# An S5 table builder with later stores, and with its TensorE part kept out of the output sums

## The chip, the cores and the metric

The kernel runs on one core of a Trainium2 chip. The metric is the device time of one execution in microseconds (us). Engines are named as the profile names them: PE is TensorE's matmul side, PEld its weight load, DVE is VectorE, ACT is ScalarE, POOL is GpSimd, and SP is the engine whose queue (SPq) issues almost all DMAs.

## The reference

Two layers work on x of 512 tokens by 1024 channels. Each layer is a SwiGLU feed-forward (FF1), a token mixer, and a second feed-forward (FF2); each has an RMS norm before and after and a shift, scale and gate from a conditioning vector:

```
c_act = silu(c)
for l in range(2):
    mod = c_act @ w_mod[l] + b_mod[l]      # nine vectors of 1024
    x = x + 0.5 * gt1 * rms_norm(swiglu(modulate(rms_norm(x), sh1, sc1)))     # FF1
    x = x + gt2 * rms_norm(mixer(modulate(rms_norm(x), sh2, sc2)))
    x = x + 0.5 * gt3 * rms_norm(swiglu(modulate(rms_norm(x), sh3, sc3)))     # FF2
swiglu(h) = (silu(h @ w_gate) * (h @ w_up)) @ w_out                            # inner width 2816
```

Half of the mixer is an S5 layer: 32 groups of 16 channels, each with a 64-dimensional complex diagonal state. Its constants (powers of the discretised A, products of these with B and C, and short-time kernels) do not depend on x. They are what the S5 table builder makes ahead of each mixer.

## The kernel before

**Products.** Every 128x128x512 product is done as three matmuls on a high and a low part of both operands (`mm3`, L266 to L268, for input products; `mmo`, L273 to L275, for output sums). A weight unit is a 128x1024 tile. Weights are streamed: `Weights.load` (L216) issues the DMA on SP's queue, ACT makes the high part (`wh`, L223, two casts), DVE the low part (`wl`, L231, two subtractions). The raw tiles have four buffers (pool `raw_p`), and the same four serve the conditioning matrix's tiles (`wm`, L141), each of which DVE multiplies by silu(c) and sums (L143).

**Feed-forward.** `ff` runs three passes over the inner width: 7, 7 and 8 blocks of 128. In a pass it makes the blocks' input products (two weight units and 48 matmuls a block, named `f00i` for FF1 of layer 0, `f02i` for FF2 of layer 0) and then the pass's output sums (`f00o`, `f02o`), 84 matmuls for each half dh of the output channels, over seven weight units in all. The four banks of half 0 come from the pool `psbg`, those of half 1 from `psmm`, which the input products also use. After the sums of pass 1, DVE adds the banks to partial sums in SBUF (`f00pt`, L567); that frees the banks. The first input product of pass 2 (block 14) takes a bank that one of these additions of half 1 frees.

**Side work.** Two generators run beside FF1 of layer 0 (tables of layer 0) and FF2 of layer 0 (tables of layer 1): `gen_mod`, the conditioning tiles, and `gen_prep`, the table builder. `tick`, which is called when an input unit or a unit of output half 1 is fetched, advances the builder by NPREP/40 steps. NPREP is 95 before. So NPREP sets how early in the program each of the builder's steps is written.

**Table builder.** It first makes small powers on DVE, then works through four chunks, `pr00` to `pr03` for layer 0 and `pr10` to `pr13` for layer 1. A chunk loads its parameters (`bc`, L689), makes `w` (L758, L761), `c0r` and `c0n`, `c`, and then `er` and `ei` (L797 to L811) on POOL. `close` of a chunk is run inside the next chunk's steps: it stores `c` (through `diag`, L749), `er` (L696) and `ei` (L697) into a DRAM table, turns w on PE into `mb` banks (L703) which ACT copies to `m` (L704), makes `g` on PE (L708, L709), whose copy `gs` ACT and DVE write (L712, L713), and stores `m` (four DMAs, L749) and `gs` (eight DMAs, L720). The parameter tile, `c0r`, `c0n` and `gs` have one buffer each. At the start of layer 0's tables, four zero stores (L682) clear the table.

**Order.** A scheduler that has its own estimate of durations decides from program order and dependencies the order in which each engine gets its instructions. Each engine, SP among them, then executes that order strictly, and waits at an instruction whose inputs are not there.

Of the kernel before, what the change touches and what calls it, by code (L numbers as in the profile page):

```python
# [16 lines left out]
T = 512  # L17
# [37 lines left out]
def trunk(ctx: ExitStack, tc: tile.TileContext, x_d, c, wmod, wun, vecs, wab, s5p, cst_d, out, depth=2):  # L55
    nc = tc.nc
# [135 lines left out]
    def tick():  # L192
        for e in list(bg):
            e[2] += e[1]
            while e[2] >= 1:
                e[2] -= 1
                if next(e[0], bg) is bg:
                    bg.remove(e)
                    break
# [205 lines left out]

    side = []
    mark = {"n": 0}

    def step():
        mark["n"] += 1  # L410
        while side:
            try:
                next(side[0])
                break
            except StopIteration:
                side.pop(0)
# [67 lines left out]
    def ff(l, s, h):  # L484
        name = f"f{l}{s}"
        part = {}

        def getw(look=LOOK, ticks=True):
            w = W.get(look)
            if ticks:  # L490
                tick()
            return w

        def evac(j, sl, pg, pu, g):
            n = sl.stop - sl.start
            sg = (half if n == HT else slot)(f"{name}sg{j}")
            ACT.activation(sg, pg[:, :n], AF.Silu)  # L497
            DVE.tensor_tensor(sg, sg, pu[:, :n], op=ALU.mult)  # L498
            after["act"] = ACT.copy(g[0][:, sl], sg)
            DVE.tensor_tensor(g[1][:, sl], sg, g[0].bitcast(F32)[:, sl], op=ALU.subtract)  # L500

        g = {}

        def newg(j):
            g[j] = (slot(f"{name}gh{j}", F32R), slot(f"{name}gl{j}", F32R))

        for p, (j0, j1) in enumerate(PASSES):
            nk = j1 - j0
            js = list(range(j0, j1))
            if p == 0 and l == 0 and s == 0:  # L510
                pp = startup(h)
                for j in range(4):
                    newg(j)
                    evac(j, FULL, pp[2 * j], pp[2 * j + 1], g[j])
                js = js[4:]
                rest()
                spread(40, mod=(gen_mod(0, range(16, 72)), 56), prep=(gen_prep(0), NPREP))
            elif p == 0:
                ws = [getw(8 - i, False) for i in range(8)]
                for j in range(4):  # L520
                    newg(j)
                for sl in HALF:
                    for grp in ((0, 1), (2, 3)):
                        pp = [mmps(f"{name}i{i}") for i in range(4)]
                        for k in range(KD):
                            for i, ps in enumerate(pp):
                                mm3(ps[:, :HT], ws[2 * grp[0] + i], k, h[k], sl, k == 0, k == KD - 1)
                                step()
                        with prio(300 if sl.start == 0 else 0):
                            for i, j in enumerate(grp):  # L530
                                evac(j, sl, pp[2 * i], pp[2 * i + 1], g[j])
                    flush()
                js = js[4:]
            if p == 2:
                o = Out(l, s, name + "o", part)
            for j in js:
                newg(j)
                pp = []
                for i in range(2):
                    w = getw()  # L540
                    ps = mmps(f"{name}i{j}")
                    for k in range(KD):
                        mm3(ps, w, k, h[k], FULL, k == 0, k == KD - 1)
                    pp.append(ps)
                evac(j, FULL, pp[0], pp[1], g[j])
            gl = [g.pop(j) for j in range(j0, j1)]
            if p < 2:
                hold = {}
                for dh in range(2):
                    acc = [(mmps if dh else bgps)(f"{name}o{dh}{tg}") for tg in range(4)]  # L550

                    def unit(kk):
                        u, j = divmod(dh * nk + kk, 2)
                        if u not in hold:
                            hold[u] = getw(ticks=dh == 1)
                        return [t[j] for t in hold[u]]

                    seq = [(kk, tg) for kk in range(nk - 3) for tg in range(4)]
                    seq += [(kk, tg) for tg in range(4) for kk in range(nk - 3, nk)]
                    for kk, tg in seq:  # L560
                        mmo(acc[tg], unit(kk), gl[kk], tg, kk == 0, kk == nk - 1)
                        if kk == nk - 1:
                            if p == 0:
                                part[tg, dh] = slot(f"{name}pt{tg}{dh}")
                                ACT.copy(part[tg, dh], acc[tg])
                            else:
                                DVE.tensor_tensor(part[tg, dh], part[tg, dh], acc[tg], op=ALU.add)  # L567
            else:
                tail_ff(o, nk, gl)
        return None if o.last else o.h  # L570

    def gen_prep(l):
# [99 lines left out]
        dram = s5d["t"]  # L672
# [5 lines left out]
        if l == 0:  # L678
            zero = slot("zero")
            POOL.memset(zero, 0.0)  # L680
            for ch in range(4):
                behind(nc.sync.dma_start(out=dram[ch, :, 0:5 * T].rearrange("p (i n) -> p i n", i=5),  # L682
                                         in_=rep(zero, 5)))
# [7 lines left out]

        def close(ch, nm, w, c, er, ei, c0r, c0n, dd, qg, diag):
            wr, wi, cr, cn = w[:, 0:256], w[:, 256:512], c[:, 0:256], c[:, 256:512]
            for i, v in enumerate((cr, cn)):
                diag(2 + i, lambda g: v.rearrange("p (q n) -> p q n", q=4)[64 * g:64 * g + 64])
            nc.sync.dma_start(out=dram[ch, :, 5 * T:6 * T], in_=er)  # L696
            nc.sync.dma_start(out=dram[ch, :, 6 * T:7 * T], in_=ei)  # L697
            yield
            mb = [slot(nm + f"m{i}") for i in range(2)]
            for i, v in enumerate((wr, wi)):  # L700
                ps = bgps(nm + f"mb{i}")
# [15 lines left out]
            for t in range(4):  # L717
                for g in range(2):
                    o = 4 * T + P * t + 64 * g
                    nc.sync.dma_start(out=dram[ch, 64 * g:64 * g + 16 * t + 16, o:o + 64],  # L720
                                               in_=gs[48 - 16 * t:64, 64 * g:64 * g + 64])
            yield

        bc = params(0)
        rest = None
        for ch in range(4):
# [19 lines left out]
            def diag(i, src, ch=ch):  # L746
                for g in range(2):
                    v = dram[ch, 64 * g:64 * g + 64, i * T:i * T + T].rearrange("p (q g n) -> p q g n", q=4, g=2)
                    nc.sync.dma_start(out=v[:, :, g], in_=src(g))  # L749
# [39 lines left out]
            cr, cn = c[:, 0:256], c[:, 256:512]  # L789
# [6 lines left out]
            er, ei = slot(nm + "er"), slot(nm + "ei")  # L796
# [3 lines left out]
            for i in range(7):  # L800
                n = 1 << i
# [18 lines left out]
        yield from rest  # L820

    s5r, s5d, neg = {}, {}, {}
    NPREP = 15 + 4 * 19 + 4

    def gen_s5(l, utc, res, nm0, chunks):
        for ch in chunks:
# [690 lines left out]
    for l in range(depth):  # L1517
# [5 lines left out]
        if l + 1 < depth:  # L1523
            load_vec(l + 1)
            spread(40, mod=(gen_mod(l + 1, range(32)), 32), prep=(gen_prep(l + 1), NPREP))
        h = ff(l, 2, h)
# [106 lines left out]
```

## Time and profile before

| | us |
|---|---|
| median of 3 runs | 2126.64 (2125.35 to 2126.95) |
| profiled execution, its own time | 2125.73 |
| its span in the trace | 2123.7 |
| PE busy | 2048.8 (96% of the span) |
| FF1 of layer 0, output sums of pass 0 / pass 1 | 38.1 / 54.0 |
| idle time of PE in FF1 of layer 0 before `f00o`, `pr01mb`, `pr01g` | 3.6, 2.2, 1.6 |

The profile is of one execution. 2.0 us of that execution's time lie outside of its span. A row of a timeline gives start and duration in us, engine, source line, operation, output and inputs, and in square brackets the idle time of the engine just before it and what ended that idle time. Line numbers are those of the kernel before.

### The profile page before, as it was taken

How to read it: one execution, taken by the hardware profiler on the slowest of the kernel's cores; microseconds unless marked ns; L12 is line 12 of the kernel's file. 1: busy time of each engine (PE TensorE's matmuls, PEld its weight loads, DVE VectorE, ACT ScalarE, POOL GpSimd, SP SyncE). 2: the span in 40 equal slices, each digit the busy share in tenths (PEclk: the TensorE clock that was granted, in tenths of full speed). 3: DMA queues.
4: the chain of work that ended last, by engine and by line, in shares of the span. 5: the costliest groups of instructions: out<-in, count | busy, mean ns of one | idle time of the engine just before them, and what ended most of it. 6: DMA issues, size and time to landing. Idle time of an engine off the chain costs nothing.

```text
span 2123.7 us, 31849 instructions
## 1 busy us (share of the span) xinstructions
PE 2048.8 (96%) x11702; PEld 1742.0 (82%) x11702; DVE 1256.7 (59%) x2936; ACT 888.4 (42%) x1954; POOL 511.4 (24%) x925
## 2 busy tenths in 40 slices
PE   7999899999789999999999999999997999999998
PEld 5888688799678988888888888888986889888886
DVE  8955666863957864555584455568558585324235
ACT  5532323575267732223362222236554674323132
POOL 4067684210421026775010000001123200000001
PEclk9999899999889999999999999999998899999999
DMA  7676667314212335555433455542132122323231
GB/s 291 231 262 194 215 191 234 109 43 147 77 56 70 124 104 179 178 193 172 136 100 129 160 171 183 180 139 80 60 130 85 46 90 90 98 91 129 70 100 50
DMA packets 109697, 286.08 MB, mean 135 GB/s; under 512 B 31154, under 2 KB 32610, under 8 KB 109540
## 3 DMA queue, kind: packets, MB, share of 16 engines
q1 hardware_dynamic: 108388, 282.39, 40.6%
q8 instruction: 92, 1.51, 0.3%
q10 hardware_dynamic: 1152, 1.65, 0.2%
q14 instruction: 65, 0.53, 0.1%
HBM read 267.59 MB, written 16.41 MB: 134 GB/s over the span
## 4 chain that ended last, share of the span: by engine, by line
PE 76%; DVE 14%; DMA 4%; ACT 3%; issue 2%; SPq 0%; POOL 0%; DVEq 0%; ACTq 0%; POOLq 0%
PE f10i L266 4%; PE f10i L267 4%; PE f10i L268 4%; PE f02i L266 4%; PE f02i L268 3%; PE f12i L268 3%; PE f12i L266 3%; PE f12i L267 3%; PE f02i L267 3%; DMA wm<-in_wmod 3%; PE f00i L267 2%; PE f00i L268 2%; PE f00i L266 2%; DVE wl L231 2%; PE f12o L273 1%
## 5 line engine op out<-in xcount | busy, mean ns | idle before, releaser
L231 DVE TENSOR_TENSOR wl<-w,wh 128x512 fp32r<-128x512 f32 x608 | 412.9, 731 | 112.3 <-ACT wh L223 111.0
L223 ACT CAST wh<-w 128x512 fp32r<-128x512 f32 x648 | 357.9, 622 | 80.5 <-DMA w<-in_wun 48.5
L143 DVE SCALAR_TENSOR_TENSOR wm<-wm,cb 128x1024 f32<-128x1024 f32 x128 | 160.7, 1255 | 229.2 <-DMA wm<-in_wmod 228.8
L266 PE MATMUL f10i<-f02ohh,wh 128*128 128x512 f32 (+1 forms) x416 | 150.0, 361 | 2.2 <-DVE f02pt L324 1.6
L267 PE MATMUL f10i<-f02ohl,wh 128*128 128x512 f32 (+1 forms) x416 | 148.9, 358 | 2.1 <-ACT f02ohl L404 2.1
L266 PE MATMUL f02i<-m0ohh,wh 128*128 128x512 f32 (+1 forms) x416 | 148.7, 360 | 0.8 <-ACT f02sg L497 0.8
L266 PE MATMUL f12i<-m1ohh,wh 128*128 128x512 f32 (+1 forms) x416 | 148.0, 358 | 0.8 <-ACT f12sg L497 0.8
L268 PE MATMUL f10i<-f02ohh,wl 128*128 128x512 f32 (+1 forms) x416 | 148.8, 358 | 0.0
L267 PE MATMUL f12i<-m1ohl,wh 128*128 128x512 f32 (+1 forms) x416 | 148.0, 357 | 0.4 <-ACT m1ohl L404 0.4
L267 PE MATMUL f02i<-m0ohl,wh 128*128 128x512 f32 (+1 forms) x416 | 148.1, 357 | 0.4 <-ACT m0ohl L404 0.4
L268 PE MATMUL f02i<-m0ohh,wl 128*128 128x512 f32 (+1 forms) x416 | 147.9, 357 | 0.2 <-DVE wl L231 0.2
L268 PE MATMUL f12i<-m1ohh,wl 128*128 128x512 f32 (+1 forms) x416 | 147.8, 357 | 0.2 <-DVE wl L231 0.2
L267 PE MATMUL f00i<-h0l,wh 128*128 128x512 f32 x344 | 135.1, 393 | 2.0 <-DVE h0l L1488 1.9
L266 PE MATMUL f00i<-h0h,wh 128*128 128x512 f32 x344 | 133.2, 393 | 3.9 <-ACT h0h L1483 3.9
L268 PE MATMUL f00i<-h0h,wl 128*128 128x512 f32 x344 | 134.4, 391 | 0.0
L330 POOL TENSOR_TENSOR f12pt<-f12pt,Gr 128x512 f32<-128x512 f32 x8 | 10.5, 1314 | 402.7 <-ACT scr L329 402.7
L231 POOL TENSOR_TENSOR wl<-w,wh 128x512 fp32r<-128x512 f32 x40 | 53.2, 1349 | 197.2 <-ACT wh L223 157.7
L330 POOL TENSOR_TENSOR f10pt<-f10pt,Gr 128x512 f32<-128x512 f32 x8 | 10.7, 1339 | 361.3 <-ACT scr L329 357.5
L498 DVE TENSOR_TENSOR f12sg<-f12sg,f12i 128x512 f32<-128x512 f32 (+1 forms) x26 | 15.7, 606 | 136.8 <-PE f12i L268 120.8
L266 PEld LDWEIGHTS f10i<-f02ohh,wh 128*128 128x128 f32 x416 | 79.2, 190 | 14.1 <-DVE f02pt L324 1.8
L267 PEld LDWEIGHTS f10i<-f02ohl,wh 128*128 128x128 f32 x416 | 79.3, 191 | 13.5 <-ACT f02ohl L404 2.4
L266 PEld LDWEIGHTS f02i<-m0ohh,wh 128*128 128x128 f32 x416 | 78.2, 189 | 12.8 <-ACT f02sg L497 1.0
(2598 smaller groups left out, 5309.0 us busy)
## 6 DMA issues: line engine op xcount, KB each, us to landing
w<-in_wun SPq DMA_DIRECT2D x324, 512.0 KB, 4.1
wm<-in_wmod SPq DMA_DIRECT2D x128, 512.0 KB, 3.9
wm<-in_wmod SPq DMA_DIRECT2D x32, 256.0 KB, 5.8
s5d<-zero SPq DMA_DIRECT2D x4, 1280.0 KB
Gr<-Gd SPq DMA_DIRECT2D x12, 256.0 KB, 4.1
x<-in_x SPq DMA_DIRECT2D x4, 512.0 KB
m0s0tb<-s5d SPq DMA_DIRECT2D x7, 256.0 KB
m0s1tb<-s5d SPq DMA_DIRECT2D x7, 256.0 KB, 5.5
```

The lines of the kernel that those rows point to most:

```text
L143: DVE.scalar_tensor_tensor(w, w, 1.0, cb, op0=ALU.mult, op1=ALU.mult, accum_out=m)
L223: ACT.copy(hi[j], raw[:, j * T:j * T + T])
L231: e.tensor_tensor(lo[j], raw[:, j * T:j * T + T], hi[j].bitcast(F32), op=ALU.subtract)
L266: PE.matmul(ps, hi, h[0][:, sl], start=start, stop=False)
L267: PE.matmul(ps, hi, h[1][:, sl], start=False, stop=False)
L268: mark["pe"] = PE.matmul(ps, lo, h[0][:, sl], start=False, stop=stop)
L273: PE.matmul(ps, gh, hi, start=start, stop=False)
L330: (POOL if self.part else DVE).tensor_tensor(y, src, self.G[dh], op=ALU.mult)
L498: DVE.tensor_tensor(sg, sg, pu[:, :n], op=ALU.mult)
```

## The change

`close` no longer begins with the stores of `c`, `er` and `ei`; they stand at its end, behind those of `m` and `gs`. Ahead of its PE part it yields as long as a flag says that the output sums of pass 0 or 1 are being written; `ff` sets the flag. NPREP goes from 95 to 109, so that the builder advances 2.725 instead of 2.375 steps a tick. Nothing is added to or taken from the work of any engine.

```
     side = []
     mark = {"n": 0}
+    phase = {"busy": False}
...
             if p < 2:
                 hold = {}
+                phase["busy"] = True
                 for dh in range(2):
...
                                 DVE.tensor_tensor(part[tg, dh], part[tg, dh], acc[tg], op=ALU.add)
+                phase["busy"] = False
             else:
                 tail_ff(o, nk, gl)
...
         def close(ch, nm, w, c, er, ei, c0r, c0n, dd, qg, diag):
             wr, wi, cr, cn = w[:, 0:256], w[:, 256:512], c[:, 0:256], c[:, 256:512]
-            for i, v in enumerate((cr, cn)):
-                diag(2 + i, lambda g: v.rearrange("p (q n) -> p q n", q=4)[64 * g:64 * g + 64])
-            nc.sync.dma_start(out=dram[ch, :, 5 * T:6 * T], in_=er)
-            nc.sync.dma_start(out=dram[ch, :, 6 * T:7 * T], in_=ei)
-            yield
+            while phase["busy"]:
+                yield
             mb = [slot(nm + f"m{i}") for i in range(2)]
...
                                                in_=gs[48 - 16 * t:64, 64 * g:64 * g + 64])
+            yield
+            for i, v in enumerate((cr, cn)):
+                diag(2 + i, lambda g: v.rearrange("p (q n) -> p q n", q=4)[64 * g:64 * g + 64])
+            nc.sync.dma_start(out=dram[ch, :, 5 * T:6 * T], in_=er)
+            nc.sync.dma_start(out=dram[ch, :, 6 * T:7 * T], in_=ei)
             yield
...
-    NPREP = 15 + 4 * 19 + 4
+    NPREP = 15 + 4 * 20 + 14
```

The scheduler's order on SP does not follow the text of `close`: in the changed kernel too, a chunk's `c`, `er` and `ei` stores stand ahead of its `m` and `gs` stores. What moves is everything of the builder against the weights around it. PE's order in FF1 of layer 0 has `pr01`'s part between the products of blocks 11 and 12 (before: inside the output sums of pass 1), `pr02`'s part between the output sums of pass 1 and block 14 (before: in block 16), and in FF2 of layer 0 `pr12`'s part right ahead of block 14 (before: in block 16). POOL's order is the same in both.

The first place is SP's queue around the `er` store of chunk 2 in FF1 of layer 0 (`wm_53` to `wm_55` are the last conditioning tiles that DVE takes around the end of pass 1's output sums). Before:

```order
L141 DMA wm_55_2929<-in_wmod 128x1024
L749 DMA s5d<-pr02c 64x4x64
L166 DMA Gd_0_2757<-Gt_0_2755 8x128
L216 DMA w_48_2965<-in_wun 128x1024
L169 DMA Gr_00_2759<-Gd_0_2757 128x512
L169 DMA Gr_01_2760<-Gd_0_2757 128x512
L141 DMA wm_56_2975<-in_wmod 128x1024
L216 DMA w_49_3033<-in_wun 128x1024
L141 DMA wm_57_3043<-in_wmod 128x1024
L696 DMA s5d<-pr02er 128x512
```

In the changed kernel, the same stretch:

```order
L216 DMA w_45_2848<-in_wun 128x1024
L141 DMA wm_52_2858<-in_wmod 128x1024
L725 DMA s5d<-pr02er 128x512
L216 DMA w_46_2926<-in_wun 128x1024
L141 DMA wm_53_2936<-in_wmod 128x1024
L141 DMA wm_54_2941<-in_wmod 128x1024
L726 DMA s5d<-pr02ei 128x512
L216 DMA w_47_3002<-in_wun 128x1024
L141 DMA wm_55_3012<-in_wmod 128x1024
```

The `er` store of chunk 2 stood behind `wm_57`; now `w_46`, `wm_53`, `wm_54`, `w_47` and `wm_55` stand behind it.

The second place is DVE at the end of pass 1's output sums (the four `f00pt` rows are the additions that free the banks of half 1, the first of them the bank of block 14). Before:

```order
L567 TENSOR_TENSOR f00pt_1488<-f00pt_1488,f00o_2556 128x512
L143 SCALAR_TENSOR_TENSOR wm_53_2835,ma_53_2837<-wm_53_2835,cb 128x1024
L567 TENSOR_TENSOR f00pt_1499<-f00pt_1499,f00o_2557 128x512
L144 TENSOR_TENSOR mod_124<-ma_53_2837,vec_122 128x1
L143 SCALAR_TENSOR_TENSOR wm_54_2840,ma_54_2842<-wm_54_2840,cb 128x1024
L567 TENSOR_TENSOR f00pt_1510<-f00pt_1510,f00o_2558 128x512
```

In the changed kernel:

```order
L143 SCALAR_TENSOR_TENSOR wm_53_2936,ma_53_2938<-wm_53_2936,cb 128x1024
L144 TENSOR_TENSOR mod_124<-ma_53_2938,vec_122 128x1
L143 SCALAR_TENSOR_TENSOR wm_54_2941,ma_54_2943<-wm_54_2941,cb 128x1024
L144 TENSOR_TENSOR mod_124<-ma_54_2943,vec_122 128x1
L143 SCALAR_TENSOR_TENSOR wm_55_3012,ma_55_3014<-wm_55_3012,cb 128x1024
L144 TENSOR_TENSOR mod_124<-ma_55_3014,vec_122 128x1
L569 TENSOR_TENSOR f00pt_1501<-f00pt_1501,f00o_2615 128x512
L569 TENSOR_TENSOR f00pt_1512<-f00pt_1512,f00o_2616 128x512
```

The first addition of half 1 stood ahead of `wm_53`; now `wm_53`, `wm_54` and `wm_55` stand ahead of it.

The third place is SP's queue around the `er` store of chunk 2 in FF2 of layer 0 (`w_138` and `w_139` are the weights of block 14). Before:

```order
L141 DMA wm_19_9950<-in_wmod 128x1024
L689 DMA pr13bc<-in_s5p 128x384
L216 DMA w_140_9984<-in_wun 128x1024
L216 DMA w_141_10087<-in_wun 128x1024
L141 DMA wm_20_10097<-in_wmod 128x1024
L216 DMA w_142_10139<-in_wun 128x1024
L749 DMA s5d<-pr12c 64x4x64 x2
L141 DMA wm_21_10149<-in_wmod 128x1024
L216 DMA w_143_10201<-in_wun 128x1024
L749 DMA s5d<-pr12c 64x4x64 x2
L141 DMA wm_22_10211<-in_wmod 128x1024
L696 DMA s5d<-pr12er 128x512
```

In the changed kernel:

```order
L692 DMA pr13bc<-in_s5p 128x384
L216 DMA w_136_9887<-in_wun 128x1024
L216 DMA w_137_9903<-in_wun 128x1024
L725 DMA s5d<-pr12er 128x512
L726 DMA s5d<-pr12ei 128x512
L216 DMA w_138_9963<-in_wun 128x1024
L141 DMA wm_18_9973<-in_wmod 128x1024
L216 DMA w_139_10017<-in_wun 128x1024
L141 DMA wm_19_10027<-in_wmod 128x1024
```

`w_138` and the tiles `wm_18` to `wm_22` stood ahead of the store; now they stand behind it. On DVE the first addition of half 1 of FF2's pass 1 stands behind `wm_22` in both kernels.

## Rows read from the trace of the kernel before

**Rows 1.** The page: busy time by engine; granted clock in 40 slices.

```profile
PE 2048.8 (96%) x11702; PEld 1742.0 (82%) x11702; DVE 1256.7 (59%) x2936; ACT 888.4 (42%) x1954; POOL 511.4 (24%) x925
PEclk9999899999889999999999999999998899999999
```

**Rows 2.** Windows: from:to, length, busy time by engine, clock, DMA share, GB/s.

```profile
core 0: us, PE busy (x) PEld busy (x) DVE busy (x) ACT busy (x) POOL busy (x), PEclk, DMA share, GB/s
105.30:143.40 38.10, 38.10 (x169) 31.53 (x168) 22.98 (x55) 12.52 (x22) 19.22 (x39) 1.00 0.84 289
221.70:275.70 54.00, 46.62 (x195) 37.26 (x193) 32.91 (x56) 15.19 (x28) 34.94 (x79) 0.87 0.60 193
254.50:261.30 6.80, 5.74 (x25) 4.93 (x26) 3.87 (x10) 3.48 (x8) 3.75 (x8) 0.50 0.41 127
```

**Rows 3.** Timeline of PE in the output sums of pass 1.

```profile
237.76 0.80 PE L273 MATMUL f00o<-wh,f00gh 128*128 128x512 f32 x1 [3.65 <-ACT wh L223]
...
275.69 0.48 PE L266 MATMUL f00i<-h0h,wh 128*128 128x512 f32 x1
```

**Rows 4.** Timeline of SP's queue in the same stretch.

```profile
221.42 0.60 SPq L749 DMA_DIRECT2D s5d<-pr01c  x1
229.69 0.33 SPq L696 DMA_DIRECT2D s5d<-pr01er  x1
...
232.97 6.59 SPq L216 DMA_DIRECT2D w<-in_wun  x5
```

**Rows 5.** Timeline of DVE at the end of that stretch.

```profile
272.88 1.23 DVE L143 SCALAR_TENSOR_TENSOR wm<-wm,cb 128x1024 f32<-128x1024 f32 x1 [1.86 <-DMA wm<-in_wmod]
```

**Rows 6.** Timeline of POOL in FF1 of layer 0.

```profile
122.38 0.83 POOL L676 TENSOR_TENSOR pr00k<-pr00bc,tfr 128x64 f32<-128x64 f32 x1 [40.00 <-DMA pr00bc<-in_s5p]
...
150.04 0.32 POOL L761 TENSOR_TENSOR pr00c<-pr00k,pr00k 128x64 f32<-128x64 f32 x1
...
206.88 0.33 POOL L676 TENSOR_TENSOR pr02k<-pr02bc,tfr 128x64 f32<-128x64 f32 x1 [10.47 <-DMA pr02bc<-in_s5p]
...
257.31 0.40 POOL L676 TENSOR_TENSOR pr02c0r<-pr02bc,cst 128x128 f32<-128x128 f32 x1 [13.44 <-PE pr01g L708]
...
270.99 0.10 POOL L797 MEMSET pr02er<- 128x4 f32 x1
...
287.59 0.74 POOL L808 TENSOR_TENSOR pr02er<-pr02y,pr02y 128x256 f32<-128x256 f32 x1
```

**Rows 7.** Timeline of SP's queue, the builder's loads in FF1 of layer 0.

```profile
94.19 6.30 SPq L682 DMA_DIRECT2D s5d<-zero  x4
...
116.86 0.42 SPq L689 DMA_DIRECT2D pr00bc<-in_s5p  x1
...
131.71 0.33 SPq L141 DMA_DIRECT2D wm<-in_wmod  x1
```

**Rows 8.** The page: DMA issues, last number us from issue to landing.

```profile
w<-in_wun SPq DMA_DIRECT2D x324, 512.0 KB, 4.1
wm<-in_wmod SPq DMA_DIRECT2D x128, 512.0 KB, 3.9
```

**Rows 9.** Timelines of POOL, SP's queue, DVE and PE in FF2 of layer 0.

```profile
869.74 0.75 POOL L676 TENSOR_TENSOR pr12k<-pr12bc,tfr 128x64 f32<-128x64 f32 x1 [8.77 <-DMA pr12bc<-in_s5p]
...
942.87 0.33 SPq L696 DMA_DIRECT2D s5d<-pr12er  x1
...
939.73 0.69 DVE L567 TENSOR_TENSOR f02pt<-f02pt,f02o 128x512 f32<-128x512 f32 x1 [0.32 <-PE f02o L275]
...
945.68 0.48 PE L266 MATMUL f02i<-m0ohh,wh 128*128 128x512 f32 x1
962.11 1.04 PE L703 MATMUL pr12mb<-cst,pr12w 128*64 128x128 f32 x8
964.12 0.50 PE L266 MATMUL f02i<-m0ohh,wh 128*128 128x512 f32 x1
```

**Rows 10.** Waits of POOL in FF2 of layer 0: total, times, longest.

```profile
POOL pr12c L758 <- issue: 6.4, 1, 6.4
```

More of the change, by code (lines that the diff above doesn't have):

```diff
@@ L407, in trunk @@
     mark = {"n": 0}
+    phase = {"busy": False}
     def step():
@@ L548, in ff @@
                 hold = {}
+                phase["busy"] = True
                 for dh in range(2):
@@ L567, in ff @@
                                 DVE.tensor_tensor(part[tg, dh], part[tg, dh], acc[tg], op=ALU.add)
+                phase["busy"] = False
             else:
@@ L693, in close @@
             wr, wi, cr, cn = w[:, 0:256], w[:, 256:512], c[:, 0:256], c[:, 256:512]
[L694 to L698, printed above, removed]
+            while phase["busy"]:
+                yield
             mb = [slot(nm + f"m{i}") for i in range(2)]
@@ L721, in close @@
                                                in_=gs[48 - 16 * t:64, 64 * g:64 * g + 64])
+            yield
+            for i, v in enumerate((cr, cn)):
+                diag(2 + i, lambda g: v.rearrange("p (q n) -> p q n", q=4)[64 * g:64 * g + 64])
+            nc.sync.dma_start(out=dram[ch, :, 5 * T:6 * T], in_=er)
+            nc.sync.dma_start(out=dram[ch, :, 6 * T:7 * T], in_=ei)
             yield
@@ L822, in trunk @@
     s5r, s5d, neg = {}, {}, {}
-    NPREP = 15 + 4 * 19 + 4
+    NPREP = 15 + 4 * 20 + 14
     def gen_s5(l, utc, res, nm0, chunks):
```

## The prediction

> **What bounds the kernel now.** I read the page first: PE is busy 96% of the span, so what can be won lies in the few stretches where its granted clock falls or it idles [rows 1]. Beside the start and the mixers the clock row shows one such place in the first feed-forward, a little past a tenth of the span. The windows then compare the output sums of pass 0 and of pass 1, which do the same 168 matmuls: 38.1 us against 54.0 us, of which 2.0 us are the table builder's PE part of chunk 1 (its like in another place runs from 962.11 to 964.12 at the full 2.4 GHz [rows 9]). So about 13.9 us are lost there, and this is what the change can touch [rows 2].
>
> The timeline of PE shows the loss in two bundles [rows 3]. First it waits 3.65 us for a weight's high part. SP's queue says why: it stood at the store of `pr01er` from 222 to 229.7, until POOL had finished, and again at `pr01ei`; five weights and tiles left only from 232.97 on [rows 4]. Then PE comes to chunk 1's part, which stands inside the sums, and waits three times for PSUM banks that DVE's additions free. Twice the clock then falls to half (1.2 GHz) for 6.8 us, once from 254.5 [rows 2]; at half clock a busy engine loses half of that, 3.4 us. The critical resource there is the chain of loads through four raw buffers in strict order on SP, and POOL, at 24% busy, decides when this queue may go on.
>
> **What the change removes.** Chunk 1's part stands between blocks 11 and 12, where no bank is awaited: the bank waits and the half clock behind them go. POOL starts earlier: `pr00bc` is now issued ahead of the zero stores, at about 94 instead of 116.86. It lands some 5.5 us later (116.86 to 122.38 [rows 6, 7]), so POOL starts at 99.3, 23 us earlier. `pr01er` is then done near 210 instead of 229.7, the weights behind it leave in time, and the 3.65 us wait goes too. Pass 1's sums should take 38.1 us again. They begin at 223.7 (2.0 us later, since chunk 1's part is now ahead) and end at 261.8; chunk 2's part follows until 263.8.
>
> **What takes its place in FF1.** The order shows two things together: `wm_53` to `wm_55` stand behind the store of `pr02er` on SP, and the addition that frees block 14's bank stands behind `wm_55` on DVE. So block 14 waits for POOL's `er` of chunk 2. When is that? In the trace of before it ends at 288.3, 165.9 us after POOL's start; 10.47 us and 13.44 us of this are waits, for `pr02bc` and for chunk 1's PE part [rows 6]. The latter goes. The loads get new places. Chunk 0's `c` ended 28 us after the start (122.38 to 150.36 [rows 6]), so now at 127.3; `pr01bc` stands behind `wm_28`, which the queue of before issues at 131.7 [rows 7], so it lands near 137.2 and costs 9.9 us. `pr02bc` costs about 4 us, and `pr03bc`, behind the stores of `pr02c` and `w_41`, about 6 us. That makes 165.9 − 23.9 + 19.9 = 161.9 us, and `er` at about 262 (99.3 + 161.9 = 261.2, and I round up for the issue in between). From 270.99 to 288.3 its last part alone takes 17.3 us [rows 6].
>
> From there: `wm_53` and `wm_54` leave 0.9 and 1.3 us later, land in 3.9 us [rows 8], and DVE takes 1.23 us for each [rows 5], which frees `wm_55`'s buffer 7.9 us behind `er`, the waits for issue between them included; 3.9 + 1.23 + 0.2 us more, and the addition of 0.69 us (as in [rows 9]) ends 13.9 us behind `er`, at 276. Block 14 starts there; it started at 275.69 before [rows 3]. The idle time, 263.8 to 276, is 12 us, longer than the 3.65 us behind which the clock fell, so I add one stretch at half clock, 3.4 us. Chunk 2's part is already done and saves its 2.0 us later. Net of FF1: +0.5 + 3.4 − 2.0 = +1.9 us. With `er` between 258 and 266 it is −2 to +6.
>
> **FF2 of layer 0.** Nothing waits there in before: block 14 starts at 945.68, right behind the sums, and the addition that frees its bank came at 939.73; the store of `pr12er` went at 942.87, and the loads of block 14 and `wm_22` were ahead of it [rows 9]. Now they are behind it. `pr12bc` is three entries earlier on SP, by my count of that queue near 859 instead of 869.74, and I take `er` at 929, that is 942.9 less 14: 10.7 us for the earlier load, and 3.2 us as half of a pause of 6.4 us on POOL that may or may not recur [rows 10], so 926 to 932. Then three loads follow one another through the buffers: `w_139`, whose subtraction frees `wm_20`'s buffer, then `wm_21`, then `wm_22`. `w_139` leaves 3.3 us behind `er`; 8.1 us for its landing (4.1 us [rows 8]) and for two casts, two subtractions and the product of `wm_18` (1.23 us, with the rest 4.0 by estimate); 5.5 us each for `wm_20` and `wm_21` (landing 3.9, product 1.23, issue 0.4); 5.8 us for `wm_22` and the addition. Sum 28.2, so block 14 can start at 957.2. PE is ready at 945.7 + 2.0 for chunk 2's part, which now stands ahead of the block. It idles 9.5 us. Net: 957.2 − 945.7 + 3.4 for the clock − 2.0 for the part that is no longer inside block 16 = +12.9 us. Bounds: nothing where `er` comes before 919, +18 with `er` at 934.
>
> **What costs nothing.** The moved stores are the same in number and size, and the table is read only in the mixer. Layer 1's feed-forwards have no builder beside them. Chunks 0 and 3 move among input products whose weights are 10 us ahead; if that cover were gone, a store like that of `pr01er` would cost its own 3.65 us wait.
>
> **Sum.** 2125.7 + 1.9 + 12.9 = 2140.5. The profiled run is 0.9 us under the median of the three, so 2141.
>
> One thing about POOL's pace is open. The same operation took 0.83 us in one place and 0.33 us in another [rows 6], so the chunks may run slower where they now lie. In the windows DVE is busy 60% and 61% of either stretch [rows 2], so I leave the pace as it was. The Trainium skill (SBUF — State Buffer, section "Who interferes with whom") says that a GpSimd instruction that reads SBUF and a VectorE instruction with two SBUF inputs take turns on one port, the later one waiting out the other. By it, with products of 1.23 us in the way, each of some ten large operations at the end of `er` could lose half of such a turn, an estimate of 6 us more in each wait and 2153 in all. The two durations agree with the rule; no row shows that the new places are worse.
>
> **The rivals.**
> - *Both waits vanish (faster).* POOL's three waits for parameters do not occur: then `er` of chunk 2 ends at 99.3 + 142 = 241, before SP would want `wm_53`, and 13.9 us are won. It decides at `er` near 249. In FF2 the same pace would bring the store before 919. Time 2125.7 − 13.9 = 2111.8. For it: the 13.9 us are really lost now. Against it: one buffer for the parameters, with each load standing in a queue that is itself paced by PE.
> - *FF1 only swaps its wait, FF2 hides its own.* Then 2125.7 + 1.9 = 2127.6. For it: PE waits for nothing there now, and its bank came 6 us early (939.73 against 945.68 [rows 9]). Against: `wm_20` to `wm_22` must pass one after another behind the store.
> - *FF1 is freed, FF2 waits:* 2125.7 − 13.9 + 12.9 = 2124.7.
> - *POOL runs slower in its new place:* 2147 and more.
>
> **Chances.** A measurement of this kernel tells about 0.2% (4.3 us) from no change. My forecast, both waits, between 2131 and 2147: 0.48. Both vanish: 0.20. FF1 swapped and FF2 hidden: 0.18, nearly all of it within 0.2%. FF1 freed and FF2 waiting: 0.09, most within. Slower still: 0.05. Faster by over 0.2%: 0.20 + 0.02 = 0.22. Within: 0.16 + 0.07 = 0.23. Slower: 0.48 + 0.05 + 0.02 = 0.55. The range 2116 to 2147 leaves out most of the faster rival and the slowest case, about 0.2. The forecast's own range is 2131 to 2147.
>
> **What would show it.** Right, if in the profile after: the output sums of pass 1 in FF1 take about 38 us with no `pr01` in them; SP waits at the store of `pr02er` until about 262; PE idles some 12 us ahead of block 14 with DVE's `f00pt` or a `wm` named as the releaser, and half a clock behind it; in FF2 PE idles 5 to 15 us ahead of `f02i` at the same block. Wrong, if `f00pt` of half 1 follows the sums at once: then POOL was earlier than I traced. If PE is idle inside the sums of pass 0, the store of `pr00er` was the one I took too lightly.

## The result and the profile after

The changed kernel took 2137.38 us (median of four runs, 2134.71 to 2140.41), the kernel before beside it 2125.99 us (2124.65 to 2126.95): a ratio of 1.0054 [1.0035, 1.0074]. It is slower, as forecast, and close to the 2141 us. A second set of runs, at the end, gave 1.0066 [1.0049, 1.0082].

The page of after, busy time by engine, stands against [rows 1]:

```profile
PE 2038.0 (96%) x11702; PEld 1734.5 (81%) x11702; DVE 1254.6 (59%) x2936; ACT 888.1 (42%) x1954; POOL 491.5 (23%) x925
```

The instruction counts are the same. PE is busy 10.8 us less (the mixers, told below) in a span 9.1 us longer (2132.8 against 2123.7 us), so it idles 19.9 us more. PE's waits in FF1 and in FF2 of layer 0 say where (us in total, times, longest; shown are those that before lacks):

```profile
PE f00i L266 <- DVE f00pt L569: 11.7, 1, 11.7
PE pr02g L708 <- DVE f00pt L569: 3.2, 1, 3.2
...
PE f02i L266 <- DVE f02pt L569: 7.4, 1, 7.4
...
PE pr12mb L703 <- DVE f02pt L569: 1.7, 1, 1.7
...
PE pr12g L708 <- DVE f02pt L569: 0.7, 1, 0.7
```

All are ahead of block 14 or in the builder's part that now precedes it; the 3.65 us of [rows 3] and the bank waits inside the sums are gone. PE's timeline at the two places:

```profile
265.95 0.28 PE L708 MATMUL pr02g<-pr02c0r,pr02w 128*64 128x32 f32 x2 [3.17 <-DVE f00pt L569]
...
279.44 0.76 PE L266 MATMUL f00i<-h0h,wh 128*128 128x512 f32 x1 [11.71 <-DVE f00pt L569]
...
958.93 0.76 PE L266 MATMUL f02i<-m0ohh,wh 128*128 128x512 f32 x1 [7.43 <-DVE f02pt L569]
```

SP's queue (start, duration; compare [rows 4, 7, 9]) shows the loads behind the `er` stores, at 260.99 and 930.90:

```profile
93.39 0.42 SPq L692 DMA_DIRECT2D pr00bc<-in_s5p  x1
...
207.78 0.33 SPq L725 DMA_DIRECT2D s5d<-pr01er  x1
...
252.00 0.33 SPq L141 DMA_DIRECT2D wm<-in_wmod  x1
260.99 0.33 SPq L725 DMA_DIRECT2D s5d<-pr02er  x1
261.37 0.42 SPq L216 DMA_DIRECT2D w<-in_wun  x1
265.23 2.28 SPq L141 DMA_DIRECT2D wm<-in_wmod  x2
...
273.51 0.33 SPq L141 DMA_DIRECT2D wm<-in_wmod  x1
...
930.90 0.33 SPq L725 DMA_DIRECT2D s5d<-pr12er  x1
```

The queue issues nothing from 252.33 to 260.99. `wm_53` and `wm_54` leave at 265.23, `wm_55` at 273.51. DVE takes `wm_55` at 277.26 and only then writes the additions that free block 14's bank. So far this is the predicted chain. But ACT and DVE tell a second thing:

```profile
263.06 1.14 ACT L223 CAST wh<-w 128x512 fp32r<-128x512 f32 x2 [16.07 <-POOL pr02ei L816]
...
263.71 1.49 DVE L231 TENSOR_TENSOR wl<-w,wh 128x512 fp32r<-128x512 f32 x2 [8.78 <-ACT wh L223]
265.12 0.68 DVE L569 TENSOR_TENSOR f00pt<-f00pt,f00o 128x512 f32<-128x512 f32 x1
...
277.26 1.23 DVE L143 SCALAR_TENSOR_TENSOR wm<-wm,cb 128x1024 f32<-128x1024 f32 x1 [3.58 <-DMA wm<-in_wmod]
...
278.61 2.47 DVE L569 TENSOR_TENSOR f00pt<-f00pt,f00o 128x512 f32<-128x512 f32 x4
```

ACT's cast of a weight that had landed waits 16.07 us for POOL's `ei` of chunk 2. The cast reads nothing of POOL's: its output tile `wh` takes one of the 71 slots (NSLOT) that weights and the builder's tiles share, and this one was POOL's scratch `y` for `er` and `ei`. This coupling of the weights to POOL the prediction had not named. It is there in FF2 too, for `ei` of that chunk 2:

```profile
932.99 0.62 ACT L223 CAST wh<-w 128x512 fp32r<-128x512 f32 x1 [12.97 <-POOL pr12ei L816]
```

The windows (length, busy time of PE, PEld, DVE, ACT, POOL, granted clock, DMA share, GB/s) give the output sums of pass 1, the idle time ahead of block 14 in FF1, and the work behind block 14's start in FF1 and in FF2:

```profile
223.70:261.70 38.00, 38.00 (x170) 31.35 (x169) 21.26 (x39) 8.81 (x16) 30.90 (x70) 1.00 0.63 214
267.40:279.40 12.00, 0.32 (x4) 0.19 (x2) 4.89 (x11) 3.29 (x7) 10.75 (x28) 0.50 0.53 169
279.40:283.30 3.90, 3.87 (x10) 3.08 (x10) 3.84 (x8) 0.00 (x0) 3.43 (x10) 0.52 0.42 138
958.90:962.50 3.60, 3.57 (x9) 2.85 (x10) 3.54 (x8) 0.00 (x0) 3.17 (x12) 0.51 0.51 148
```

The sums take 38.0 us against 54.0 [rows 2]. The time won there is lost right behind them, and FF2 loses without having won anything.

Two stage lengths compare all runs: FF1 of layer 0 from the first output sum of pass 0 to the first of pass 2 (`f00o` to `f00od`), and FF2 of layer 0 from its first input product to the same point (`f02i` to `f02od`). Each is from the run's profiled execution; the ratio is to the kernel before in the same series. The kernel before had a median of 2125.99 us beside the first row of after, 2120.90 beside the kernels with pace 109, with pace 95, with 109 in FF1 alone and with stores on POOL, 2120.46 beside 109 in FF2 alone, own scratch tile and own tiles, and 2122.14 beside the rest. Its stages were traced in the first series alone.

| kernel | FF1 | FF2 | median us | ratio |
|---|---|---|---|---|
| before | 261.8 | 331.7 | 2125.99 | 1 |
| after | 265.5 | 343.5 | 2137.38 | 1.0054 [1.0035, 1.0074] |
| after, second time | 266.4 | 343.4 | 2136.29 | 1.0066 [1.0049, 1.0082] |
| before, pace 109 | 260.1 | 345.4 | 2136.58 | 1.0061 [1.0041, 1.0080] |
| after, pace 95 | 259.5 | 331.9 | 2121.85 | 1.0002 [0.9991, 1.0014] |
| after, 109 in FF1 alone | 267.0 | 332.7 | 2127.22 | 1.0031 [1.0018, 1.0043] |
| after, 109 in FF2 alone | 259.8 | 342.9 | 2132.14 | 1.0053 [1.0036, 1.0070] |
| after, `er`/`ei` stores on POOL | 266.6 | 339.7 | 2137.43 | 1.0067 [1.0048, 1.0085] |
| after, own scratch tile | 265.3 | 349.9 | 2142.21 (one run) | |
| after, own tiles, stores on POOL | 337.4 | 393.9 | 2260.11 | 1.0662 [1.0646, 1.0678] |
| before, the same | 324.0 | 395.1 | 2254.49 | 1.0636 [1.0620, 1.0652] |
| after, decoupled | 288.3 | 355.1 | 2168.85 | 1.0220 [1.0203, 1.0236] |
| before, decoupled | 263.0 | 342.0 | 2131.77 | 1.0051 [1.0033, 1.0070] |
| after, pace 95, decoupled | 279.1 | 339.8 | 2150.21 | 1.0131 [1.0108, 1.0153] |

### The profile page after: what moved, and what is told of

Its sections match the earlier page's. It is cut to its first block, busy times and chain, and to the rows that moved or that the text cites. A ratio compares the mean times of both kernels' runs of the same rounds, so it can differ in the third digit from the quotient of the medians.

```text
span 2132.8 us, 31829 instructions
## 1 busy us (share of the span) xinstructions
PE 2038.0 (96%) x11702; PEld 1734.5 (81%) x11702; DVE 1254.6 (59%) x2936; ACT 888.1 (42%) x1954; POOL 491.5 (23%) x925
## 4 chain that ended last, share of the span: by engine, by line
PE 72%; DVE 14%; POOL 4%; ACT 3%; DMA 3%; issue 3%; SPq 0%; DVEq 0%; ACTq 0%; POOLq 0%
PE f10i L266 4%; PE f10i L267 4%; PE f10i L268 4%; PE f02i L266 4%; PE f02i L268 3%; PE f02i L267 3%; PE f12i L268 3%; PE f12i L266 3%; PE f12i L267 3%; PE f00i L267 2%; PE f00i L266 2%; PE f00i L268 2%; DMA wm<-in_wmod 2%; DVE wl L231 2%; PE f12o L273 1%
## 5 line engine op out<-in xcount | busy, mean ns | idle before, releaser
L231 DVE TENSOR_TENSOR wl<-w,wh 128x512 fp32r<-128x512 f32 x608 | 407.8, 723 | 126.1 <-ACT wh L223 112.6
L143 DVE SCALAR_TENSOR_TENSOR wm<-wm,cb 128x1024 f32<-128x1024 f32 x128 | 161.9, 1266 | 220.6 <-DMA wm<-in_wmod 220.4
L266 PE MATMUL f00i<-h0h,wh 128*128 128x512 f32 x344 | 133.7, 394 | 15.0 <-DVE f00pt L569 11.7
```

Of the source, the lines that this page charges most:

```text
L143: DVE.scalar_tensor_tensor(w, w, 1.0, cb, op0=ALU.mult, op1=ALU.mult, accum_out=m)
L231: e.tensor_tensor(lo[j], raw[:, j * T:j * T + T], hi[j].bitcast(F32), op=ALU.subtract)
L266: PE.matmul(ps, hi, h[0][:, sl], start=start, stop=False)
```

## The experiments

The theory after the result: the pace (NPREP) writes `er` of chunk 2 ahead of loads that block 14 needs, and SP's queue stands at this store until POOL is done. Rivals: the flag and the moved stores do it, whatever the pace; the shared slots do it; or DVE's new order alone does it, with the additions behind `wm_55`.

**Which part of the change.** The kernel before with the new pace alone, and the changed kernel with the old pace:

```
-    NPREP = 15 + 4 * 19 + 4
+    NPREP = 15 + 4 * 20 + 14
```

> The kernel before with NPREP 109 alone; close() as before, no flag. Theory (SP stands at the er store of chunk 2 until POOL is done, and the bank of block 14 is freed behind conditioning tiles that are queued behind that store): the er stores stand as early on SP as in the changed kernel, so both waits ahead of block 14 come back. In FF1 the first addition of half 1 stands behind wm_54 and not wm_55, so block 14 starts some 6 us earlier than in the changed kernel: about 273 instead of 279.4. In FF2 chunk 2's PE part lies inside the output sums and may add bank waits. Time 2130 to 2138. Rival (the flag and the later stores cause the loss): like the kernel before or faster, 2112 to 2126.

> The changed kernel with NPREP 95 (flag and later stores kept). Theory: the er store of chunk 2 stands behind wm_55 on SP again, so nothing ahead of block 14 waits for it; chunk 1's PE part is out of the output sums, so its bank waits and the half clock behind them go, while the late pr01er store still holds the weights (3.65 us and half a clock behind it). FF2 as in the kernel before. Time 2114 to 2121. Rival (the flag or the text order of the stores makes the new waits): PE idles about 10 us ahead of block 14 here too, 2126 to 2140.

The new pace alone gives 1.0061, the whole loss. Its main waits in FF1 and in FF2:

```profile
PE f00i L266 <- DVE f00pt L567: 10.0, 1, 10.0
...
PE pr12mb L703 <- POOL pr13k L676: 6.0, 1, 6.0
PE pr12g L708 <- DVE f02pt L567: 3.1, 1, 3.1
```

In FF1 block 14 starts at 272.50, as expected (273), and the sums have no wait left. In FF2 the expected wait ahead of block 14 did not come: chunk 2's part, which stands inside the sums there, meets the late loads first. SP stood 16.6 us at the store of `pr12er`, until 931.75.

With the old pace the rest of the change makes no difference that can be told (1.0002 [0.9991, 1.0014]). The gain that I expected of it did not come, since in FF1 a new wait takes the old one's place, while FF2 has none:

```profile
PE f00i L266 <- DVE f00pt L569: 6.7, 1, 6.7
PE f00o L273 <- DVE pr01gs L713: 2.2, 1, 2.2
...
269.82 1.23 DVE L143 SCALAR_TENSOR_TENSOR wm<-wm,cb 128x1024 f32<-128x1024 f32 x1 [4.70 <-DMA wm<-in_wmod]
...
284.40 0.38 SPq L725 DMA_DIRECT2D s5d<-pr02er  x1
```

I had expected nothing to hold block 14 here. It starts at 272.00, so chunk 2's `er` store, at 284.40, has no part in its wait of 6.7 us. The additions of half 1 stand behind conditioning products in this kernel too, and the last of these products came at 269.82. So DVE's order costs something without that store, where the loads run late. What made them late was not separated: SP stood 8.6 us at the store of `pr01er` (until 226.84), and the twelve stores of `pr01m` and `pr01gs` follow (231.65 to 240.33).

One line of the table doesn't fit "the pace alone": in FF1 it costs the kernel before nothing (260.1), while it costs the changed one 6 us (265.5 against 259.5). In FF1 the pace also takes away the loss inside the sums, which the kernel before has and the changed text avoids but for 2.2 us without it; in FF2, where there is no such loss, the pace is enough.

**Which stage.** The new pace in one stage at a time (the diff is that of FF1 alone; in FF2 alone, the same number stands in FF1's call):

```
-            spread(40, mod=(gen_mod(l + 1, range(32)), 32), prep=(gen_prep(l + 1), NPREP))
+            spread(40, mod=(gen_mod(l + 1, range(32)), 32), prep=(gen_prep(l + 1), 95))
```

> The changed kernel with NPREP 109 for the tables of layer 0 (FF1) and 95 for those of layer 1 (FF2). Theory: FF1 as in the changed kernel (PE idles about 11 us ahead of block 14), FF2 as in the kernel before (nothing waits ahead of its block 14). Against the kernel before +3 us in FF1 and nothing in FF2: 2126 to 2131. Rival (FF2's wait comes from the flag or from the later stores): FF2 loses its 12 us here too, 2136 to 2142.

> The changed kernel with NPREP 95 for the tables of layer 0 (FF1) and 109 for those of layer 1 (FF2), the counterpart of the run that changed FF1 alone. If the two stages are independent: FF1 as with the old pace (2 to 3 us faster than before), FF2 as in the changed kernel (PE idle 9 to 10 us at chunk 2's part and ahead of block 14, the stage 11 to 12 us longer); against the kernel before on the same chip +7 to +11 us. Rival (FF2's loss depends on what FF1 did): FF2 within 3 us of the kernel before.

Each stage keeps its own loss: FF1 alone 267.0 and 332.7, FF2 alone 259.8 and 342.9. The two ratios less 1 (0.0031 and 0.0053) add up to 0.0084, a little more than the 0.0054 and 0.0066 of the whole.

**Which coupling.** First SP's store is taken away: `er` and `ei` are stored by POOL's own queue, which is in order with their making.

```
-            nc.sync.dma_start(out=dram[ch, :, 5 * T:6 * T], in_=er)
-            nc.sync.dma_start(out=dram[ch, :, 6 * T:7 * T], in_=ei)
+            nc.gpsimd.dma_start(out=dram[ch, :, 5 * T:6 * T], in_=er)
+            nc.gpsimd.dma_start(out=dram[ch, :, 6 * T:7 * T], in_=ei)
```

> The changed kernel with the er and ei stores of every chunk issued from POOL's queue, where they stand right behind the instruction that makes them; all else as in the changed kernel, DVE's order too (first addition of half 1 behind wm_55, and behind wm_22 in FF2). Theory: SP never stands at an er store; block 14 of FF1 starts at 264 to 267 and PE does not idle there for over 2 us, the same in FF2; time 2110 to 2116. Rival (DVE's order is what costs: the additions stand behind tiles that come at the loads' own pace): PE still idles 5 us or more ahead of block 14 in FF1 and FF2, time 2128 to 2140.

FF2 is 3.8 us shorter, FF1 is not, and the time shows no gain (1.0067): the theory of SP's store alone falls. SP's queue no longer holds the store, and stands all the same; ACT shows for what:

```profile
SPq L216 <- DVE wl L231: 19.4, 4, 14.0
```

```profile
259.22 0.61 POOL L725 DMA_DIRECT2D s5d<-pr02er  x1
...
260.64 1.14 ACT L223 CAST wh<-w 128x512 fp32r<-128x512 f32 x2 [16.01 <-POOL pr02ei L816]
```

Then the other one: the scratch gets a tile of its own, so that no weight waits for its slot, and the store stays on SP.

```
-NSLOT = 71
+NSLOT = 70
...
-            y1, y2 = slot(nm + "y1"), slot(nm + "y2")
+            yy = pw_p.tile([P, T], F32, tag="yy", name=nm + "yy")
+            y1, y2 = yy[:, :HT], yy[:, HT:]
```

> The changed kernel with one fixed tile for POOL's two scratch tiles y1 and y2 and one arena slot less; SP's order around the er store of chunk 2 and DVE's order at the end of pass 1 are as in the changed kernel. In it the weights of block 15 no longer wait for a slot that POOL frees at the end of chunk 2's ei; the er store still stands ahead of w_46, wm_53 and wm_54 on SP. Theory (either of the two couplings is enough): PE still idles 8 to 12 us ahead of block 14 in FF1, now released by tiles that SP issued behind the store. Rival (the arena slot was the only cause): block 14 starts within 3 us of chunk 2's PE part.

The cast's wait for POOL is gone, and PE waits as before, now for the queue (one run, 2142.21 us):

```profile
264.83 0.33 SPq L725 DMA_DIRECT2D s5d<-pr02er  x1
...
265.74 0.88 SPq L141 DMA_DIRECT2D wm<-in_wmod  x2
...
270.71 1.23 DVE L143 SCALAR_TENSOR_TENSOR wm<-wm,cb 128x1024 f32<-128x1024 f32 x1 [10.23 <-DMA wm<-in_wmod]
...
PE f00i L266 <- DVE f00pt L569: 15.6, 1, 15.6
```

So either coupling is enough, and taking one away shows only the other. FF2 shows the same: with the stores on POOL the cast waits 13.8 us for `pr12ei` (until 935.53), with the scratch tile SP stands at the store of `pr12er` until 935.55. The next pair takes both: `w`, `c`, `er`, `ei` and the scratch in six tiles of their own (NSLOT 65), and the stores on POOL's queue, in either kernel.

```
-            w = slot(nm + "w")
+            w = pw_p.tile([P, T], F32, tag="pw", name=nm + "w", bufs=2)
...
-            c = slot(nm + "c")
+            c = pw_p.tile([P, T], F32, tag="pc", name=nm + "c")
...
-            er, ei = slot(nm + "er"), slot(nm + "ei")
+            er, ei = [pw_p.tile([P, T], F32, tag="p" + v, name=nm + v) for v in ("er", "ei")]
```

> The changed kernel with the builder's w, c, er, ei and scratch in six fixed tiles of their own (65 arena slots instead of 71) and with the er and ei stores on POOL's queue: no weight waits for a slot that POOL frees, and SP stands at no er store. DVE's order at the ends of pass 1 is as in the changed kernel. Theory (both couplings together make the wait): PE idles under 3 us ahead of block 14 in FF1 and in FF2; FF1 about 12 us and FF2 about 11 us shorter than in the changed kernel, so 10 to 15 us faster than the kernel before on the same chip, unless the mixers lose by the fewer slots. Rival (DVE's order, the additions behind wm_55 and wm_22, is enough by itself): PE still idles 5 us or more at both places.

> The kernel before (old pace, chunk 1's PE part inside the output sums of pass 1) with the same six fixed tiles and the er and ei stores on POOL's queue. Theory: its 3.65 us wait for weights in pass 1's sums goes, with one of the two stretches at half clock; the two bank waits at chunk 1's part may stay, since the additions stand behind wm tiles there. FF1 5 to 9 us shorter than before, FF2 unchanged, so 4 to 9 us faster than the kernel before unless the mixers lose by the fewer slots. Rival (the loss in the kernel before is the bank wait alone): under 3 us.

They were 140 and 134 us slower, and tell nothing of block 14. With no slot to wait for, the orders of POOL and of SP were remade, and SP stands at what the builder has left in its queue, in the changed kernel longest at a store of `c` (L754):

```profile
SPq L754 <- POOL pr01k L679: 73.3, 1, 73.3
```

In the kernel before with the same tiles SP stands longest at a load of parameters (39.5 us) and at a store of `c` (22.7 us). That the shared slots had been a brake on how early these stand in the queue is my reading; no run shows it by itself. The six slots fewer cost the first mixer nothing (291.7 us from `m0p` to `f02i`, 292.8 before).

Last, SP's queue is freed of all that POOL makes or takes: beside the six tiles, the parameter loads and the stores of `c`, `er` and `ei` go to POOL's queue, and `dd` is made by POOL.

```
-            behind(nc.sync.dma_start(out=t, in_=s5p[l, :, 48 + 384 * ch:432 + 384 * ch]))
+            behind(nc.gpsimd.dma_start(out=t, in_=s5p[l, :, 48 + 384 * ch:432 + 384 * ch]))
...
-                    nc.sync.dma_start(out=v[:, :, g], in_=src(g))
+                    (nc.gpsimd if i > 1 else nc.sync).dma_start(out=v[:, :, g], in_=src(g))
...
-            DVE.tensor_tensor(qg(dd[32:64]), qg(bc[32:64, S_D2:S_D2 + P]),
+            POOL.tensor_tensor(qg(dd[32:64]), qg(bc[32:64, S_D2:S_D2 + P]),
```

> The changed kernel with every coupling of the weights' path to POOL's table work cut: the builder's w, c, er, ei and scratch in six fixed tiles (65 arena slots), its parameter loads and its c, er and ei stores on POOL's queue, and the small product dd on POOL instead of DVE. The order of PE and of DVE (first addition of half 1 behind wm_55, and behind wm_22 in FF2) is that of the changed kernel. Theory (block 14 waits for POOL through the arena and through SP's queue, and not for DVE's order as such): PE idles under 4 us ahead of block 14 in FF1 and in FF2; FF1 10 to 15 us and FF2 9 to 12 us shorter than in the changed kernel; against the kernel before on the same chip 8 to 15 us faster. Rival (DVE's order is enough): PE idles 5 us or more at both places and the time is that of the kernel before or longer.

> The kernel before (NPREP 95, no flag, chunk 1's PE part inside the output sums of pass 1) with the same cuts. Theory: the 3.65 us wait for a weight and the half clock behind it go; the bank waits at chunk 1's PE part shrink or stay, since DVE's additions stand behind wm tiles. FF1 5 to 14 us shorter than before, FF2 within 2 us; 4 to 14 us faster than the kernel before on the same chip. Rival (the wait for the weight has another source than POOL): under 3 us.

> The changed kernel with NPREP 95 and the same cuts: flag and later stores kept. Theory: once POOL no longer holds the weights, the pace does not matter, so it is within 3 us of the changed kernel with the same cuts, and both are the fastest of all. Rival (the early pace is what pays once the couplings are gone): 4 us or more slower than that.

PE's longest waits of the changed kernel so decoupled, in FF1 and in FF2, and the one in FF1 of the kernel before and of the old pace (7.3 and 5.6 us in FF2):

```profile
PE pr01g L708 <- POOL pr01c0r L679: 37.4, 1, 37.4
...
PE pr11g L708 <- POOL pr11c0r L679: 20.8, 1, 20.8
```

```profile
PE pr01g L708 <- POOL pr01c0r L676: 11.7, 1, 11.7
```

```profile
PE pr01g L708 <- POOL pr01c0r L679: 28.0, 1, 28.0
```

The idle time ahead of block 14 is gone in both stages. The time was worse in all three, where I had expected gains in all three; and the old pace, which I had expected within 3 us of the new one, is 18.6 us faster here. The reason is in POOL's order, which the new tiles and queues remade. In the changed kernel so decoupled:

```profile
214.64 0.72 POOL L814 TENSOR_TENSOR pr02er<-pr02yy 128x256 f32<-128x256 f32 x1
...
238.71 0.40 POOL L679 TENSOR_TENSOR pr01c0r<-pr01bc,cst 128x128 f32<-128x128 f32 x1
```

POOL makes `er` of chunk 2 ahead of `c0r` of chunk 1, which the changed kernel has at 170.81; PE, in its old order, waits for this `c0r`. So the three runs do not isolate the couplings. `er` of chunk 2 is done at 215.36, 88 us before pass 1's sums end (303.16), and could have held no load there by either coupling. What the first of them does show is DVE's order: the additions of half 1 still stand behind four conditioning products (the last from 300.50 to 301.73), the additions end at 304.32, and block 14 starts at 305.12 without a wait. Where the loads keep up, as here, that order alone costs nothing. The changed kernel without the couplings and with POOL's order kept was not run.

**Once more, the changed kernel.**

> The changed kernel once more, beside the kernel before on this chip, where that takes 2120.5 instead of 2126. The stages say +3 us in FF1 and +12 us in FF2, and the mixers, which the change leaves alone, vary by several us from run to run. Expected 2130 to 2137 here, 10 to 15 us slower than the kernel before; a difference under 8 us would mean that the mixers give part of it back in most runs.

1.0066, with block 14's waits at 11.6 and 7.4 us: the same picture.

No run beat the kernel before; the changed kernel with the old pace equals it.

## Why the prediction was right

**Pass 1's sums.** Right: 38.0 us, from 223.7 to 261.7, and neither `pr01` nor a wait in them. `pr00bc` left at 93.39 (94 was said), `pr01er` at 207.78 (210), `pr02er` at 260.99 (262). One reading behind it was wrong: in the kernel before PE waits at chunk 1's part twice (2.2 and 1.6 us), not three times. The 13.9 us do not hang on it.

**When `er` of chunk 2 comes.** The time was hit and its terms were not, which is luck. POOL from its first operation, or from chunk 2's first, to the end of that `er`, before and after (the fifth busy time is POOL's):

```profile
122.38:288.33 165.95, 158.57 (x703) 130.00 (x702) 100.75 (x181) 43.09 (x81) 126.69 (x285) 0.96 0.65 206
869.74:942.84 73.10, 73.10 (x339) 60.56 (x338) 43.42 (x75) 20.37 (x38) 58.66 (x139) 1.00 0.59 191
```

```profile
99.04:260.96 161.92, 161.92 (x746) 134.12 (x745) 102.99 (x213) 45.20 (x84) 125.68 (x285) 1.00 0.70 236
861.65:930.87 69.22, 69.22 (x321) 57.37 (x320) 34.00 (x55) 18.16 (x35) 49.26 (x139) 1.00 0.45 143
```

In FF1 the stretch is 161.9 us, as forecast, but with 24.4 us of waits for 19.9: 11.9, 7.2 and 3.9 us for the three loads (9.9, 4 and 6 were said) and 1.4 us with no releaser named. The forecast also left a wait of 2.05 us for `pr03bc` in the 165.9 us and added its own term for the same load. The other 2.5 us are shorter work and shorter pauses. In FF2 POOL starts on chunk 2 at 861.65 and not at 859, and the pause of 6.4 us does not recur; but POOL then waits 16.15 us for `pr13bc` (0.58 us before), which the forecast did not have, and works 9.4 us less. POOL's order is not the same in both kernels, as the section on the change has it: in after the first products of chunk 2 stand inside `er` of chunk 1 (192.11 in 176.42 to 207.75).

**The wait in FF1.** The mechanism was right and its chain too short. Block 14 starts at 279.44, not 276, 18.4 us behind `er` and not 13.9. The step that failed is "`wm_53` and `wm_54` leave 0.9 and 1.3 us later": they left 4.2 us behind `er` (265.23 less 260.99), because the raw buffer that they need is read by the subtraction at 263.71, that waits for the cast at 263.06, and the cast for POOL's `ei`. This is the slot coupling, 3.3 us of the 4.5. The same subtraction stands ahead of the last addition of half 0 (265.12), hence the 3.17 us inside chunk 2's part. FF1 lost 3.7 us where +1.9 was forecast.

**The clock.** Over-sized: 3.4 us for each stretch at half clock. The granted clock was at 0.50 during FF1's idle time already; of PE's work only 3.9 us (FF1) and 3.6 us (FF2) ran at about half, which costs half of that, 1.9 and 1.8 us. This error of 1.5 us a stage offsets part of the one above. (The net of FF1 also counts +0.5 us where its own times, 276 and 275.69, give +0.3.)

**The wait in FF2.** Right in its length: `er` at 930.90 (929 was said, 926 to 932), and block 14 28.0 us behind it (28.2). PE idled 7.43 us rather than 9.5, since chunk 2's part waited 1.66 and 0.67 us for banks of its own. The slot coupling acts here too, but the cast is let go at 932.99, no later than SP's queue (store of `ei` at 932.98), and `w_138` to `wm_19` leave from 933.40 to 935.24, about when the forecast had `w_139` (3.5 us behind `er` for 3.3); so leaving it out cost the forecast nothing here. FF2 lost 11.8 us where +12.9 was forecast.

**The sum.** +14.8 forecast, +15.5 in the two stages, and +9.0 between the two profiled executions. The difference came back in the mixers, where both kernels have the same instructions in the same order. Windows of the two mixers, before and after (the second window takes in the output sums ahead of that mixer, from 1408 to 1454 in before):

```profile
412.60:705.40 292.80, 272.62 (x2225) 240.31 (x2224) 192.24 (x521) 178.92 (x445) 58.24 (x56) 0.94 0.25 80
1408.40:1748.70 340.30, 321.10 (x2436) 280.48 (x2435) 227.10 (x607) 202.44 (x496) 67.06 (x62) 0.93 0.26 84
```

```profile
415.90:706.30 290.40, 268.80 (x2225) 237.63 (x2225) 191.84 (x521) 178.89 (x446) 58.10 (x56) 0.95 0.25 81
1421.60:1757.80 336.20, 314.56 (x2436) 275.04 (x2434) 227.14 (x607) 202.50 (x496) 66.95 (x62) 0.95 0.26 85
```

The same matmuls take 3.8 and 6.5 us less of PE's time at a higher granted clock; the prediction had put the mixers at nothing. In the second mixer this goes with the change. From its first `m1p` to the first `f12i`, the three profiles with the old pace in FF2 (before, pace 95, 109 in FF1 alone) have 294.0 to 294.2 us, the five with the changed FF2 (after twice, 109 in FF2 alone, stores on POOL, own scratch tile) 289.8 to 290.1 us. Why the granted clock differs there is not shown. The first mixer, from 290.2 to 294.3 us in these runs and the kernel before with pace 109, shows no such split. The medians differ by 11.4 us and, the second time, by 14.2 us (2136.29 less 2122.14), both below the sum of the stages.

**The rivals.** That both waits vanish needed `er` of chunk 2 near 249; it came at 260.99. That FF2 hides its wait is refuted by the 7.4 us there and by the run with the pace in FF2 alone (1.0053). That FF1 is freed is refuted by the 11.7 us. That POOL runs slower in its new place is refuted by its busy time up to that `er`, 125.68 us for 126.69 in FF1 and 49.26 for 58.66 in FF2. The estimate of 6 us more in each wait, worked out by the rule of the Trainium skill (SBUF — State Buffer, section "Who interferes with whom"), was over-sized: the last part of `er` alone took 18.95 us in FF1 (242.01 to 260.96) for 17.3 before, 1.6 us more.

**What stays open.** How far the slot and the store each delay block 14 when both act was not separated beyond the 3.3 us. That the loss goes with both couplings gone and all else kept was not shown, since every kernel without both had POOL's order remade. And a kernel in which POOL's real pace decides the order was not tried.

## What to carry to other kernels

Before a helper's work is written earlier, look up when its slowest engine has it done, and list every in-order queue on which an instruction for it now stands ahead of the main stream: stores on the load queue, but also casts that wait for a tile slot, and matmuls. Tiles from one shared pool of slots couple streams that share no data; taking away one coupling shows nothing while another is left, and where both are taken away, look at what this did to the engines' orders. And a change in pace that empties one busy stretch is to be judged by the next strict wait, not by the stretch.

## What the runs showed of the hardware

A product on POOL that began inside a DVE product of 128x1024 ended only as the latter did. In FF1 of after, one such pair and POOL's next operation of the same form:

```profile
265.94 1.21 DVE L143 SCALAR_TENSOR_TENSOR wm<-wm,cb 128x1024 f32<-128x1024 f32 x1
...
266.07 1.22 POOL L679 TENSOR_TENSOR pr03k<-pr03w,ta1i 128x64 f32<-128x64 f32 x1
267.26 0.29 POOL L679 TENSOR_TENSOR pr03k<-pr03w,ta1r 128x64 f32<-128x64 f32 x1
```

0.29 us became 1.22 us, and POOL went on as DVE's product ended (267.15; 266.07 + 1.22 = 267.29). The next meeting, at 269.04, gave 1.25 us. Either cost about 0.9 us, since POOL began just behind DVE; the 0.83 us of [rows 6], 0.5 us over the 0.33 us of the same operation elsewhere, began in the middle of such a product (DVE from 121.83 to 123.06). Here the rule of the Trainium skill (the section named above) does show. In the run with the `er` and `ei` stores on POOL, issuing such a store kept POOL 0.61 us; on SP's queue it took 0.33 us.
